# Down projections summed without the residual and without 1/rms, with x kept in device memory until the last part

## The chip, the cores and the metric

The kernel runs on one core of a Trainium2 chip. The time is the device time of one execution in microseconds, and the figure for a kernel is the median of its timed runs. Besides, one execution is recorded by the hardware profiler; its rows are quoted as they stand. The engines are named as in the profile: PE is TensorE's matrix multiplication, PEld its loading of weights, DVE is VectorE, ACT ScalarE, POOL GpSimd and SP SyncE. SP does no arithmetic here; it issues transfers, one after the other. POOL issues the transfers that add what they bring to what lies at their target.

## The reference, cut to what matters

One inference step of a decoder with two layers: 512 prompt positions and 8 sample positions, model width 1024. Layer 0 has a causal pooling mixer, layer 1 sliding-window attention, and each layer has a feed-forward network (FFN) ahead of the mixer and one behind it, four in all:

```python
def _rmsnorm(x, g):
    y = xf * lax.rsqrt(jnp.mean(xf * xf, axis=-1, keepdims=True) + EPS)
    return (y * g.astype(jnp.float32)).astype(x.dtype)

def _swiglu(x, wg, wu, wd):
    return (jax.nn.silu(x @ wg) * (x @ wu)) @ wd
...
        x = x + 0.5 * _swiglu(_rmsnorm(x, norm_g[l, 0]), ffn_w_gate[l, 0], ffn_w_up[l, 0], ffn_w_down[l, 0])
        h = _rmsnorm(x, norm_g[l, 1])
        ... mixer ...
        x = x + out
        x = x + 0.5 * _swiglu(_rmsnorm(x, norm_g[l, 2]), ffn_w_gate[l, 1], ffn_w_up[l, 1], ffn_w_down[l, 1])
```

wg and wu (Gate and Up) are 1024 x 2816, wd (Down) is 2816 x 1024. Everything is in float32.

## The kernel before

**Data.** The residual stream x stays in on-chip memory, transposed: eight tiles `x[0]` to `x[7]`, each 128 features by 520 tokens (512 and 8), 266 KB. A tile is worked on in two halves of 260 tokens. `R`, of the same shape, holds 1/rms of each token in all partitions. Since 1/rms is one factor for each token, Up's result is left without it, and the sum of Down is multiplied by `R` instead.

**Arithmetic.** A float32 matrix is split into a high and a low part (`wh` and `wl` for weights, the weight's high part by ScalarE at L260, the low one by VectorE at L261; `split`, L315, for the moving side), and a product is three matmuls: high by high, high by low, low by high. One matmul moves 128 x 260.

**An FFN** (`ffn`, L803). The 2816 hidden features are 22 tiles of 128, in three parts of 8, 8 and 6 (`PARTS`, L26). A part first makes its hidden tiles (Gate, Up, Silu, product) and then its Down, which sums over the hidden features of this part alone; so each part adds a third of the Down sum. The first two to four tiles of an FFN are computed plainly, the others by a Strassen–Winograd scheme of seven products in place of eight (`strassen_tile`), which needs sums of weight blocks. The Downs of parts 0 and 1 use the seven products as well (`strassen_down`, L727), for four pairs of x tiles, `x[2i]` and `x[2i+1]`. The Down of the last part, of six tiles, is plain; `add` (L827) puts its result into x.

**A pair in `strassen_down`.** `head`, `second`, `third` and `rest` issue the seven products (`product`, L556, matmul at L563, four weight tiles of three matmuls each) and, between them, the copies `sa` and `sb` on ScalarE (L736, L738, L744). In `third`, the sum `u` is built (L751), multiplied by `R` (L752), and `x[2i]` takes −0.5 times it (L753); `sb` takes the next product (L755). In `rest`, the two halves are multiplied by `R` (L760, L762) and `x[2i+1]` takes 0.5 times the result (L763). The signs come from the hidden values, which are kept negated. The `rest` of one pair is issued behind the head of the next, that of the last pair behind the first products of the next part's tile.

**Weights.** SP loads raw weights (L334) into three buffers (`rawp`), each as soon as VectorE's split at L261 has set a buffer free. For the Strassen sums, SP loads a block a second time into a buffer `S`; POOL adds a block to it by an accumulating transfer (L191), and another block to a block of raw (L192); VectorE makes two further sums (L197, L201). The splits run up to five pieces ahead of the products. POOL's transfers are issued in order, as SP's are.

**Order.** A scheduler reorders the instructions of an engine by its own estimate of their times, except those put into `later`, which keep the order of the text. Weight loads on SP are of that kind; the instructions of `strassen_down` on VectorE are not.

**Start of FFN 1.** Behind the pooling mixer, whose last updates of x are at L1099, the text issues on SP: a copy of the pooling state to its output (L1142), copies of the key and value caches (L1145), a load of the attention sinks (L1149) and eight small loads that spread them over partitions (L1151), all in `later`. L1180 to L1182 on VectorE turn these loads into the form that the attention uses; the text has them behind FFN 1, the scheduler puts them into its first tiles.

**Device memory.** The pool `kvp` (L1156) holds tiles in device memory, so far for keys and values.

Of the kernel before, what the change touches and what calls it, by code (L numbers as in the profile page):

```python
# [11 lines left out]
F32 = mybir.dt.float32  # L12
F32R = mybir.dt.float32r
I32 = mybir.dt.int32
AF = mybir.ActivationFunctionType
ALU = mybir.AluOpType
AX = mybir.AxisListType

P = 128
D = 1024  # L20
KT = 8
# [3 lines left out]
TOK = SP + NS  # L25
TW = TOK + NS  # L26
H = TOK // 2
PARTS = (8, 8, 6)
# [252 lines left out]
def yoco_step(ctx, tc, ins, outs):  # L281
# [9 lines left out]
    splp = ctx.enter_context(tc.tile_pool(name="splp", bufs=6))  # L291
    psp = ctx.enter_context(tc.tile_pool(name="psp", bufs=4, space=bass.MemoryType.PSUM))
    cnt = [0]

# [175 lines left out]
    def hcols(t, hf):  # L470
        return t[:, hf * H : (hf + 1) * H]


    def halves(t):
        return t.rearrange("p (h c) -> p h c", h=2)
# [250 lines left out]

    def strassen_down(tmp, hs):  # L727

# [17 lines left out]
        def third(i):  # L746
            a, c, sa, sb = st[i]
            product(b["B21"], c[:, 0, :])
            product(b["B22"], c[:, 1, :], True)
            u = tmp.tile([P, TOK], F32, tag="u", name="u", bufs=nu[0])  # L750
            V.tensor_tensor(halves(u), halves(sa), c[:, :, :H], op=ALU.add)  # L751
            V.tensor_tensor(u, u, R, op=ALU.mult)  # L752
            V.scalar_tensor_tensor(x[2 * i], u, -0.5, x[2 * i], op0=ALU.mult, op1=ALU.add)  # L753
            product(b["T3"], a, True)
            V.tensor_tensor(sb, sb, a[:, :H], op=ALU.add)  # L755

        def rest(i):
            a, c, sa, sb = st.pop(i)
            u = tmp.tile([P, TOK], F32, tag="u", name="u", bufs=nu[0])
            V.tensor_tensor(hcols(u, 1), sb, hcols(R, 1), op=ALU.mult)  # L760
            product(b["T4"], a, True)
            V.tensor_tensor(hcols(u, 0), a[:, :H], hcols(R, 0), op=ALU.mult)  # L762
            V.scalar_tensor_tensor(x[2 * i + 1], u, 0.5, x[2 * i + 1], op0=ALU.mult, op1=ALU.add)  # L763

# [38 lines left out]
    def ffn(fi, tmp, mov, hooks, tt, tags, after, before_last=None, first=None, by_parts=None, hold=False):  # L803

        j = 0
        for pi, n in enumerate(PARTS):
# [3 lines left out]
            for _ in range(n):  # L810
                if j == 0 and first is not None:
                    plain_end(tmp, *first, hs)
                elif j < NPL[fi]:
                    plain_tile(tmp, mov, hs, hooks)
                else:
                    while hooks:
                        hooks.pop(0)()
                    strassen_tile(tmp, mov, tt, hs)
                j += 1
                W.pin = lambda ins: ins  # L820
            if seven:
                strassen_down(tmp, hs)
                continue
            nk = (n + 1) // 2
            rest = NH if last and by_parts is not None else 0

            def add(m, bank, hfs):  # L827
                c = slice(hfs[0] * H, (hfs[-1] + 1) * H)
                u = tmp.tile([P, TOK], F32, tag="u", name="u", bufs=nu[0])[:, c]
                parts = lambda z: z.rearrange("p (h c) -> p h c", c=H)  # L830
                pin = later if last and hold and m == KT - 1 else seq
                pin(V.tensor_tensor(parts(u), bank[:, hfs[0] : hfs[-1] + 1, :H], parts(R[:, c]), op=ALU.mult))
                pin(V.scalar_tensor_tensor(x[m][:, c], u, -0.5, x[m][:, c], op0=ALU.mult, op1=ALU.add))

# [14 lines left out]
            for m in range(KT - rest):  # L849
                if m > 1:  # L850
                    banks[m] = duo()
                    mm_tile(hs, banks[m])
                add(m, banks[m], (0, 1))
                if last:
# [300 lines left out]

    kvp = ctx.enter_context(tc.tile_pool(name="kvp", bufs=1, space=bass.MemoryType.DRAM))  # L1156
    kT_kept = [kvp.tile([P, SP], F32, name=f"kT_kept{g}") for g in range(2)]
# [720 lines left out]
```

## Time and profile before

| | |
|---|---|
| median of 3 runs | 1652.23 us |
| lowest and highest | 1649.66 and 1653.12 us |
| profiled execution | 1657.26 us |
| its span | 1655.5 us |
| mean granted TensorE clock | 0.990 |

The stages of the profiled execution, by the first and last matmuls of each (us from the start of the span, rounded):

| | Down, part 0 | Down, part 1 | Down, last part |
|---|---|---|---|
| FFN 0 (from 9) | 108 to 146 | 230 to 268 | 325 to 372 |
| FFN 1 (from 401) | 492 to 530 | 615 to 653 | 712 to 757 |
| FFN 2 (from 776) | 864 to 902 | 986 to 1024 | 1084 to 1127 |
| FFN 3 (from 1301) | 1383 to 1421 | 1505 to 1543 | 1602 to 1656 |

The pooling mixer lies between 372 and 401 us, the attention between 1127 and 1301 us.

How to read the rows. A group row has the line, the engine, the operation, target and sources with their shapes, the count, the busy time and the mean duration in ns, and behind the second bar the idle time of the engine just before these instructions with what ended it. A row of a stretch has from and to, the length, and for each engine the busy time with the count of instructions, then the granted clock, the share of time for which the sixteen transfer engines were busy, and GB/s. A row of the timeline has start, duration, engine, line, operation and operands, and in square brackets the idle time before it with the releaser. A row of waits has who waited, for whom, and in total, times and longest. A transfer row has the queue, the count, KB each, and the median time from issue to landing.

### The profile page before, as it was taken

To read this page: it belongs to the slowest core of one execution; us is meant where nothing else is said; L and a number is where in the kernel's file an instruction comes from. 1 tells how busy PE (TensorE), PEld (TensorE's weight loads), DVE (VectorE), ACT (ScalarE), POOL (GpSimd) and SP (SyncE) were. 2 spreads that over 40 slices of the span, in tenths; PEclk is the share of its full clock that TensorE was granted. 3 is DMA by queue.
4 is the path that set the end of the run, shared out by engine and by line. 5 is a ranking of instruction groups with operands and counts; after the bars stand their busy time and mean duration, and the time that the engine had idled before them with its cause. 6 is when DMAs were issued, how large, how long until landed. Compare 5 with 4: busy or idle time off the path is not lost.

```text
span 1655.5 us, 34978 instructions
## 1 busy us (share of the span) xinstructions
PE 1624.3 (98%) x13386; PEld 1607.8 (97%) x13386; DVE 1421.8 (86%) x2817; ACT 980.1 (59%) x2032; POOL 228.9 (14%) x304
## 2 busy tenths in 40 slices
PE   9999999999999999999999999999989999999997
PEld 9999999999999999999999999999989999999997
DVE  6999999887899999888899989886786799999886
ACT  5665665566665565655655665655785565565555
POOL 1111111000111111100211111101110111111100
PEclk9999999999999999999999999999979999999999
DMA  8577878752587887744787877753222567787851
GB/s 225 119 174 180 183 175 176 192 158 87 127 181 176 179 185 176 163 134 103 186 186 178 182 175 173 170 181 91 59 50 75 126 142 176 179 184 173 178 139 52
DMA packets 377363, 254.62 MB, mean 154 GB/s; under 512 B 13134, under 2 KB 343878, under 8 KB 377156
## 3 DMA queue, kind: packets, MB, share of 16 engines
q1 hardware_dynamic: 339390, 187.30, 40.9%
q0 software_dynamic: 34048, 60.00, 22.7%
q10 hardware_dynamic: 3758, 5.09, 1.0%
q8 instruction: 105, 1.72, 0.4%
q14 instruction: 62, 0.51, 0.1%
HBM read 189.76 MB, written 6.11 MB: 118 GB/s over the span
## 4 chain that ended last, share of the span: by engine, by line
PE 90%; DVE 3%; ACT 3%; DMA 1%; issue 1%; POOL 0%; SPq 0%; DVEq 0%; ACTq 0%; POOLq 0%
PE ps L563 64%; PE ps L535 20%; ACT wh L260 1%; DVE wl L261 1%; PE ps L1464 1%; PE ps L1061 1%; DMA pr<-in_bands_dram 1%; PE ps L1086 1%; ACT sm L1408 1%; PE ps L1377 0%; PE ps L1433 0%; PE ps L494 0%; PE ps L1752 0%; PE ps L1759 0%; DMA raw<-in_ffn_w_gate_dram 0%
## 5 line engine op out<-in xcount | busy, mean ns | idle before, releaser
L260 ACT ACTIVATE wh<-raw 128x512 fp32r<-128x512 f32 (+1 forms) x794 | 465.3, 619 | 262.7 <-PE ps L535 81.3
L261 DVE TENSOR_TENSOR wl<-raw,wh 128x512 fp32r<-128x512 f32 (+1 forms) x794 | 518.0, 675 | 71.1 <-ACT wh L260 69.1
L563 PE MATMUL ps<-th,wh 128*128 128x260 f32 x1216 | 343.7, 284 | 1.5 <-ACT wh L260 1.2
L563 PE MATMUL ps<-th,wl 128*128 128x260 f32 x1216 | 342.4, 282 | 0.6 <-DVE wl L261 0.6
L563 PE MATMUL ps<-tl,wh 128*128 128x260 f32 x1216 | 342.3, 282 | 0.0
L563 PE MATMUL ps<-xh,wh 128*128 128x260 f32 x896 | 253.6, 284 | 3.3 <-ACT sb L707 1.8
L563 PE MATMUL ps<-xl,wh 128*128 128x260 f32 x896 | 251.6, 282 | 0.0
L563 PE MATMUL ps<-xh,wl 128*128 128x260 f32 x896 | 250.5, 282 | 0.5 <-DVE wl L261 0.4
L192 POOL DMA_DIRECT2D raw<-raw x108 | 93.1, 862 | 1046.8 <-DVE wl L261 283.5
L563 PEld LDWEIGHTS ps<-th,wh 128*128 128x128 f32 x1216 | 228.4, 188 | 3.7 <-ACT wh L260 2.5
L563 PEld LDWEIGHTS ps<-th,wl 128*128 128x128 f32 x1216 | 228.8, 188 | 0.8 <-DVE wl L261 0.8
L563 PEld LDWEIGHTS ps<-tl,wh 128*128 128x128 f32 x1216 | 229.0, 188 | 0.0
L563 PE MATMUL ps<-hh,wh 128*128 128x260 f32 x656 | 184.7, 285 | 2.4 <-ACT wh L260 1.8
L563 PE MATMUL ps<-hl,wh 128*128 128x260 f32 x656 | 183.8, 283 | 0.2 <-DVE hl L320 0.2
L563 PE MATMUL ps<-hh,wl 128*128 128x260 f32 x656 | 183.1, 282 | 0.0
L563 PEld LDWEIGHTS ps<-xh,wh 128*128 128x128 f32 x896 | 168.3, 188 | 5.3 <-ACT sb L707 2.2
L563 PEld LDWEIGHTS ps<-xh,wl 128*128 128x128 f32 x896 | 168.1, 188 | 0.9 <-DVE wl L261 0.9
L563 PEld LDWEIGHTS ps<-xl,wh 128*128 128x128 f32 x896 | 168.4, 188 | 0.0
L563 PEld LDWEIGHTS ps<-hh,wh 128*128 128x128 f32 x656 | 123.0, 188 | 4.3 <-ACT wh L260 2.8
L563 PEld LDWEIGHTS ps<-hl,wh 128*128 128x128 f32 x656 | 123.3, 188 | 0.4 <-DVE hl L320 0.4
L563 PEld LDWEIGHTS ps<-hh,wl 128*128 128x128 f32 x656 | 123.0, 188 | 0.0
L535 PE MATMUL ps<-hh,wh 128*128 128x260 f32 x572 | 116.3, 285 | 0.6 <-ACT vtok L1245 0.6
(331 smaller groups left out, 3595.2 us busy)
## 6 DMA issues: line engine op xcount, KB each, us to landing
raw<-in_ffn_w_gate_dram SPq DMA_DIRECT2D x87, 512.0 KB, 5.6
raw<-in_ffn_w_up_dram SPq DMA_DIRECT2D x87, 512.0 KB, 5.6
raw<-in_ffn_w_down_dram SPq DMA_DIRECT2D x128, 256.0 KB, 4.4
raw<-raw POOLq DMA_DIRECT2D x108, 256.0 KB, 3.5
S<-raw POOLq DMA_DIRECT2D x108, 256.0 KB, 4.6
S<-in_ffn_w_up_dram SPq DMA_DIRECT2D x76, 256.0 KB, 6.2
raw<-in_ffn_w_down_dram SPq DMA_DIRECT2D x16, 768.0 KB, 4.5
S<-in_ffn_w_down_dram SPq DMA_DIRECT2D x32, 256.0 KB, 4.5
```

The source lines that it names most:

```text
L192: G.dma_start(blk(raw, 2, 1), blk(raw, 1, 1), accum_op=ALU.add)
L260: pin(nc.scalar.activation(dh, src, AF.Copy))
L261: pin(nc.vector.tensor_tensor(dl, src, dh.bitcast(F32), op=ALU.subtract))
L535: ins = T.matmul(banks[:, hf, :H], a[:, kk, :], hcols(b, hf), start=(first and i == 0), stop=(last and i == 2),)
L563: T.matmul(bank[:, :H], a[:, kk, :], b, start=(not more and kk == 0 and i == 0), stop=(kk == 3 and i == 2), skip_group_check=more,)
L1061: T.matmul(o, a[:, s], b[:, kk, :], start=(n == 0), stop=(n == 5))
L1086: T.matmul(po[:, half * 256 : half * 256 + 256], z[:, tau, c], b, start=(i == 0), stop=(i == len(lst) - 1),)
L1408: S.activation(z, z, AF.Exp, scale=-1.0, bias=nm[:, i : i + 1], accum_out=self.den[:, i : i + 1])
L1464: T.matmul(po[:, bi * 256 : (bi + 1) * 256], a, p_[:, kc_], start=(n == 0), stop=(n == 3 * len(kts) - 1),)
```

## The change

For each FFN, eight tiles `kept[0]` to `kept[7]` in device memory take a copy of x. SP stores them, two behind each of the tiles 4 to 7 of the text. From then on x itself holds the bare sum of the Downs: part 0 writes it (`first`), without the sign and the factor, so that no `R` and no old x is needed; part 1 adds to it or subtracts from it. In the last part, `restore` turns x[m] into −0.5 · x[m] · `R` on VectorE, and an accumulating transfer on POOL adds `kept[m]`. The Down of the last part adds to x as it did.

```diff
+    kvp = ctx.enter_context(tc.tile_pool(name="kvp", bufs=1, space=bass.MemoryType.DRAM))
...
-    def strassen_down(tmp, hs):
+    def strassen_down(tmp, hs, first):
...
-            u = tmp.tile([P, TOK], F32, tag="u", name="u", bufs=nu[0])
+            y = x[2 * i]
+            u = y if first else tmp.tile([P, TOK], F32, tag="u", name="u", bufs=nu[0])
             V.tensor_tensor(halves(u), halves(sa), c[:, :, :H], op=ALU.add)
-            V.tensor_tensor(u, u, R, op=ALU.mult)
-            V.scalar_tensor_tensor(x[2 * i], u, -0.5, x[2 * i], op0=ALU.mult, op1=ALU.add)
+            if not first:
+                V.tensor_tensor(y, y, u, op=ALU.add)
             product(b["T3"], a, True)
-            V.tensor_tensor(sb, sb, a[:, :H], op=ALU.add)
+            if first:
+                V.scalar_tensor_tensor(hcols(x[2 * i + 1], 1), sb, -1.0, a[:, :H], op0=ALU.mult, op1=ALU.subtract)
+            else:
+                V.tensor_tensor(sb, sb, a[:, :H], op=ALU.add)
 
         def rest(i):
             a, c, sa, sb = st.pop(i)
-            u = tmp.tile([P, TOK], F32, tag="u", name="u", bufs=nu[0])
-            V.tensor_tensor(hcols(u, 1), sb, hcols(R, 1), op=ALU.mult)
+            y = x[2 * i + 1]
+            if not first:
+                V.tensor_tensor(hcols(y, 1), hcols(y, 1), sb, op=ALU.subtract)
             product(b["T4"], a, True)
-            V.tensor_tensor(hcols(u, 0), a[:, :H], hcols(R, 0), op=ALU.mult)
-            V.scalar_tensor_tensor(x[2 * i + 1], u, 0.5, x[2 * i + 1], op0=ALU.mult, op1=ALU.add)
+            if first:
+                S.activation(hcols(y, 0), a[:, :H], AF.Copy, scale=-1.0)
+            else:
+                V.tensor_tensor(hcols(y, 0), hcols(y, 0), a[:, :H], op=ALU.subtract)
...
-        j = 0
+        j, kept = 0, [kvp.tile([P, TOK], F32, name=f"x{fi}_{k}") for k in range(KT)]
+
+        def restore(m):
+            V.scalar_tensor_tensor(x[m], x[m], -0.5, R, op0=ALU.mult, op1=ALU.mult)
+            nc.gpsimd.dma_start(x[m], kept[m], accum_op=ALU.add)
+
...
                 j += 1
                 W.pin = lambda ins: ins
+                if 4 <= j < 8:
+                    for k in (2 * j - 8, 2 * j - 7):
+                        nc.sync.dma_start(kept[k], x[k])
+                if last:
+                    i = j - sum(PARTS) + n
+                    for m in range(KT * (i - 1) // n, KT * i // n):
+                        restore(m)
             if seven:
-                strassen_down(tmp, hs)
+                strassen_down(tmp, hs, pi == 0)
                 continue
```

`add` keeps its two operations (multiply by `R`, add −0.5 times it to x) and loses a parameter that had one value only. Neither the stores, nor the restoring multiplication, nor the accumulating transfer is in `later`.

More of the change, by code (lines that the diff above doesn't have):

```diff
@@ L825, in ffn, with add @@
             rest = NH if last and by_parts is not None else 0
[L827 to L833, printed above, removed]
+            def add(m, bank):
+                u = tmp.tile([P, TOK], F32, tag="u", name="u", bufs=nu[0])
+                pin = later if hold and m == KT - 1 else seq
+                pin(V.tensor_tensor(halves(u), bank[:, :, :H], halves(R), op=ALU.mult))
+                pin(V.scalar_tensor_tensor(x[m], u, -0.5, x[m], op0=ALU.mult, op1=ALU.add))
             if last and hold:
@@ L852, in ffn @@
                     mm_tile(hs, banks[m])
-                add(m, banks[m], (0, 1))
+                add(m, banks[m])
                 if last:
@@ L1153, in yoco_step @@
         ffn(1, tmp, mov2, start_hooks(tmp, 2, tt, 2), tt, HH, deferred(N_KV, tmp, "g", XX, movk))
-    kvp = ctx.enter_context(tc.tile_pool(name="kvp", bufs=1, space=bass.MemoryType.DRAM))
     kT_kept = [kvp.tile([P, SP], F32, name=f"kT_kept{g}") for g in range(2)]
```

## The prediction

> **What bounds the kernel now.** I read the busy table of the page first, then the chain of work that ended last.
>
> ```profile
> span 1655.5 us, 34978 instructions
> PE 1624.3 (98%) x13386; PEld 1607.8 (97%) x13386; DVE 1421.8 (86%) x2817; ACT 980.1 (59%) x2032; POOL 228.9 (14%) x304
> PE 90%; DVE 3%; ACT 3%; DMA 1%; issue 1%; POOL 0%; SPq 0%; DVEq 0%; ACTq 0%; POOLq 0%
> ```
>
> TensorE is busy for 98% of the span and carries 90% of the chain. The change removes no matmul, so it can gain only where TensorE waits now, and lose where it waits newly. The 1655.5 us of the span stand in an execution of 1657.26 us (1.76 around it), and that is 5.0 us above the median of 1652.23. I work out a difference on the profiled execution and add it to the median.
>
> The third view is the busy time of each engine in stretches: one stretch in which TensorE never waits, then the four Downs of part 0 (each cut in two where x is first updated, at 121.4, 506, 877 and 1398 us), then the four Downs of part 1.
>
> ```profile
> core 0: us, PE busy (x) PEld busy (x) DVE busy (x) ACT busy (x) POOL busy (x), PEclk, DMA share, GB/s
> 150.00:188.00 38.00, 38.00 (x320) 38.00 (x319) 34.50 (x65) 23.36 (x47) 6.99 (x8) 1.00 0.82 171
> 108.00:121.40 13.40, 13.07 (x104) 12.45 (x104) 13.33 (x27) 9.63 (x21) 1.74 (x3) 1.00 0.62 148
> 121.40:146.00 24.60, 24.60 (x207) 24.60 (x206) 22.99 (x43) 10.71 (x22) 5.15 (x6) 1.00 0.85 191
> 492.00:506.00 14.00, 14.00 (x119) 14.00 (x119) 13.21 (x26) 9.57 (x22) 1.72 (x2) 1.00 0.74 185
> 506.00:530.00 24.00, 23.98 (x199) 23.73 (x198) 23.14 (x43) 10.23 (x21) 5.21 (x6) 1.00 0.81 183
> 864.00:877.00 13.00, 12.72 (x103) 12.19 (x102) 12.93 (x26) 9.44 (x21) 1.72 (x2) 1.00 0.55 129
> 877.00:902.00 25.00, 25.00 (x211) 25.00 (x211) 23.47 (x43) 11.06 (x23) 5.18 (x6) 1.00 0.87 197
> 1383.00:1398.00 15.00, 14.52 (x119) 14.10 (x118) 14.04 (x28) 10.17 (x22) 2.58 (x3) 1.00 0.69 166
> 1398.00:1421.00 23.00, 23.00 (x195) 23.00 (x194) 22.02 (x41) 9.76 (x21) 4.36 (x5) 1.00 0.85 176
> ...
> 230.00:268.00 38.00, 37.31 (x311) 37.10 (x310) 36.34 (x69) 20.24 (x42) 6.90 (x8) 1.00 0.80 184
> 615.00:653.00 38.00, 36.51 (x300) 35.89 (x299) 35.44 (x67) 20.26 (x43) 6.91 (x8) 1.00 0.76 181
> 986.00:1024.00 38.00, 36.16 (x297) 35.51 (x296) 35.45 (x66) 20.87 (x43) 6.79 (x8) 1.00 0.74 174
> 1505.00:1543.00 38.00, 37.72 (x308) 36.94 (x308) 36.75 (x68) 20.60 (x44) 6.93 (x8) 1.00 0.75 180
> ```
>
> The numbers in brackets count matmuls. With no wait, 320 fit into 38 us, 0.119 us each. By that spacing the head parts of Down 0 hold 9, 0, 6 and 7 fewer than fit and the remainders 0, 3, 0 and 0: 25 slots, 3.0 us (33 slots, 3.9 us, if each of the eight stretches also counts one matmul cut by its edge). The Downs of part 1 miss 9, 20, 23 and 12 against 320: 64 slots, 7.6 us. VectorE is the fullest engine beside TensorE in these stretches (13.33 of 13.40, 12.93 of 13.00, 36.75 of 38), and the transfer engines are busy 0.74 to 0.87 of the time.
>
> **The change, part by part.** The groups of instructions of the Down function, alike in shape, are the price list (x32: four pairs, two parts, four FFNs):
>
> ```profile
> L751 DVE TENSOR_TENSOR u<-sa,ps 128x520 f32<-128x520 f32 x32 | 22.1, 690 | 5.6 <-PE ps L563 4.1 <-ACT sa L744 1.4
> L752 DVE TENSOR_TENSOR u<-u,R 128x520 f32<-128x520 f32 x32 | 22.3, 696 | 0.4
> L753 DVE SCALAR_TENSOR_TENSOR x<-u,x 128x520 f32<-128x520 f32 x32 | 22.2, 692 | 0.0
> L755 DVE TENSOR_TENSOR sb<-sb,ps 128x260 f32<-128x260 f32 x32 | 13.4, 419 | 2.8 <-PE ps L563 2.8
> L760 DVE TENSOR_TENSOR u<-sb,R 128x260 f32<-128x260 f32 x32 | 13.5, 421 | 0.0
> L762 DVE TENSOR_TENSOR u<-ps,R 128x260 f32<-128x260 f32 x32 | 13.6, 426 | 5.2 <-PE ps L563 5.0
> L763 DVE SCALAR_TENSOR_TENSOR x<-u,x 128x520 f32<-128x520 f32 x32 | 22.2, 695 | 0.3
> L736 ACT COPY sa<-ps 128x260 f32<-128x260 f32 x32 | 11.3, 371 | 21.1 <-PE ps L563 21.1
> ```
>
> *VectorE in Down 0.* A pair costs 0.690+0.696+0.692+0.419+0.421+0.426+0.695 = 4.04 us now. Afterwards the sum goes straight into x (0.69) and one half-width subtraction remains (0.42): 1.11. That is 2.93 less a pair, 11.7 an FFN, 47 us in all. But the first of it comes at the first x update, and the slots are lost ahead of that: 22 of 25. I take the 3 behind it as won (0.36 us) and a quarter of the 22 (0.65 us), since a shorter block moves some weight splits forward: −1.0 us. Bounds: 0 and −3.9.
>
> *ScalarE in Down 0.* Sixteen new half-width copies, by the nearest row (0.371) 5.9 us in all. ScalarE works about 10 us of each 24 behind the heads, and its free time hides them: nothing (0.37 us each on the path, 5.9 in all, if the left half of x were waited for at once; nobody reads it before part 1's Down).
>
> *VectorE in Down 1.* A pair becomes 0.690 (u), 0.69 (x plus u), 0.419 and two half-width subtractions of 0.42: 2.64. The restoring multiplications are issued in the last part of the program text, but in the changed program's instruction order they stand in Down 1 and the tile behind it: two a pair, 1.39. Together 4.03 against 4.04: nothing moves there. What VectorE gains, it gains in Down 0 alone.
>
> *Transfers.* Stores first: 32 of 266 KB on SP. Then 32 accumulating ones on POOL, whose nearest kin are the two of the weight sums.
>
> ```profile
> q1 hardware_dynamic: 339390, 187.30, 40.9%
> q0 software_dynamic: 34048, 60.00, 22.7%
> ...
> raw<-raw POOLq DMA_DIRECT2D x108, 256.0 KB, 3.5
> S<-raw POOLq DMA_DIRECT2D x108, 256.0 KB, 4.6
> ```
>
> The plain queue moves 187.30 MB in 40.9% of 1655.5 us: a store takes the engines for 0.96 us, 7.7 us an FFN, in the tiles at its start, where the engines are half idle (the 403 to 423 us row below, 0.46): nothing; in a full stretch it would be priced like the additions that follow. POOL's queue is almost only the 216 accumulating transfers: 22.7% of 1655.5 over 216 is 1.74 us of all sixteen engines each, 13.9 us for the eight of an FFN. In the changed order they stand among the weight sums of four chunks (x0, x1, a chunk, x2, x3, a chunk, x4 …), so they fall into the some 38 us of Down 1. Its four rows leave 0.20, 0.24, 0.26 and 0.25 of 38 us free, 9.0 us in the mean: 4.9 us too little. What that costs is bounded by 0 (the loads run ahead) and the whole backlog, 4 × 4.9 = 19.6 us. The nearest rows are a stretch that saturates today:
>
> ```profile
> 288.00:298.00 10.00, 10.00 (x86) 10.00 (x85) 7.23 (x14) 5.22 (x11) 1.96 (x3) 1.00 1.03 209
> 298.00:308.00 10.00, 10.00 (x85) 10.00 (x85) 9.73 (x18) 6.56 (x14) 0.85 (x2) 1.00 0.95 209
> ...
> 318.00:328.00 10.00, 9.98 (x83) 9.76 (x82) 9.83 (x19) 7.33 (x16) 0.00 (x0) 1.00 0.48 141
> ```
>
> Twenty microseconds at 1.03 and 0.95 are followed by 83 matmuls in place of 86: 3 × 0.119 = 0.36 us. I take 0.4 an FFN, +1.5 us.
>
> The Trainium skill speaks against the size of that term: in "DMA: Bandwidth & Descriptors", section "Anatomy of one DMA — SWDGE (gpsimd) path", a transfer issued by GpSimd takes about 2.0 us fixed and its bytes over 436 GB/s. By that, as an estimate, a 266 KB addition moves data for 0.6 us, eight would fit into the free time, and the sum would be 1.5 us lower; but POOL's own rows show 1.74 us of occupancy and 3.5 to 4.6 to landing, and those decide.
>
> *SP's queue at the start of FFN 1.* In the changed order all eight stores of FFN 1 stand ahead of the state and cache copies (L1142, L1145), the sink loads (L1151) and the next S load. SP takes its issues in order, so all of them wait for the last x of the pooling mixer. Four issues and instructions in order of time, with start and duration, and two more stretches:
>
> ```profile
> 368.88 1.08 SPq L1142 DMA_DIRECT2D out_dram<-in_state_pool_dram  x1
> ...
> 371.95 15.66 SPq L1151 DMA_DIRECT2D sink_s<-in_attn_sinks_dram  x8
> 401.89 0.74 DVE L1099 SCALAR_TENSOR_TENSOR x<-ps,gT,x 128x512 f32<-128x512 f32 x1
> ...
> 421.27 0.15 DVE L1182 TENSOR_SCALAR sink_s<-sink_s 128x1 f32<-128x1 f32 x1
> ...
> 403.00:423.00 20.00, 20.00 (x170) 20.00 (x169) 16.49 (x46) 13.12 (x25) 1.90 (x3) 1.00 0.46 103
> 438.00:449.00 11.00, 8.99 (x69) 8.15 (x68) 9.47 (x20) 8.05 (x17) 0.00 (x0) 1.00 0.00 1
> ```
>
> These issues last from 368.88 to 387.61, 18.7 us. Begun at 402.6 they end at 421.4 at the earliest, and the last sink then has to land; VectorE, in order, stands at L1182, 421.27 today, and behind it are the weight splits. The S load, issued last, is late for its sums as well. VectorE would be some 3 us late, part of which its pauses take up. Eleven microseconds later TensorE already loses slots (69 of 93). I take half of the 3, +1.5 us, between 0 and +5 (the 3 in full, and 2 more for sums that follow the late S load, an estimate).
>
> *SP elsewhere.* In FFNs 0, 2 and 3 the stores stand between weight loads.
>
> ```profile
> SPq L334 <- DVE wl L261: 854.0, 118, 24.1
> ```
>
> SP waits there 854 us for buffers that VectorE's splits set free, 7.2 us a time, and the x in question are made before those: 0. If a store waited longer than its gate, each microsecond would shorten the lead of the loads behind it by as much.
>
> Sum: −1.0 + 1.5 + 1.5 = +2.0 us; 1652.23 + 2.0 = **1654.2 us**.
>
> **Rivals.** *A, the transfers decide.* The backlog of 4.9 us an FFN meets weight sums that already arrive last:
>
> ```profile
> ACT wh L260 <- DMA S<-raw: 28.8, 13, 3.2
> ```
>
> ScalarE waits 28.8 us for these sums, in 13 places. If half the backlog reaches TensorE it is 4 × 2.45 = 9.8 us; with −1.0 and +1.5 that is +10.3: 1662.5 us, slower. For it speaks the missing 4.9 us; against it the 0.36 us after saturation. It decides from about 0.7 us lost an FFN (0.4 and a quarter of the 1.3 that part my forecast from 1655.5). The Trainium skill's "Perfetto Trace Analysis", "Identifying the Most-Contended Engine", would have transfers judged by memory bandwidth, not by occupancy of sixteen engines, which would make A unlikely; the fall to 83 behind the share of 1.03 and 0.95 speaks the other way.
>
> *B, the relief reaches TensorE.* If an emptier Down 0 keeps the heads fed (3.9 us) and shorter blocks in Down 1 (u and one addition, 1.38 us, where three operations of 2.08 stood) win a third of the 7.6 us there, 2.5, and transfers and the start of FFN 1 cost nothing, it is −6.4: 1645.8 us. For it: VectorE is full where the slots are lost. Against: the losses lie ahead of what is removed.
>
> *C, the work is only moved.* No relief in Down 0, and the restores, put by the scheduler among the splits of Down 1, raise its loss by half: +3.8, 1656.0 us. For it: VectorE at 36.75 of 38. Against: the count of operations a pair is no higher.
>
> **How the numbers follow.** The measurement tells about 0.2%, 3.3 us, from no change: faster is below 1648.9, slower above 1655.5. The forecast has 0.46 (faster 0.02, same 0.27, slower 0.17; its own range is 1651 to 1658, from −1.0 with no costs to +5 at the start of FFN 1 and +1.5), A 0.25 (slower), B 0.20 (faster 0.18, same 0.02), C 0.09 (same 0.04, slower 0.05). Totals 0.20, 0.33, 0.47. The range reaches below B and just past A's price, 1645.5 to 1664; the far halves of A and B, some 0.18, stay outside.
>
> **What would show it.** VectorE's busy time falls by some 47 us, all of it in the Downs of part 0, whose head stretches still miss slots. In the Downs of part 1 the transfer share rises towards 1, the matmul counts stay within a few of 311, 300, 297 and 308. The sinks of FFN 1 are issued after 402 us, L1182 moves to about 424, and 438 to 449 loses more. I am wrong if Down 1 falls by tens of matmuls (A), if the heads of Down 0 fill (B), or if a wait shows elsewhere: a store that holds SP's weight loads, or an addition that holds POOL's weight sums past their due time.

## The result, and the profile after

| | before | changed |
|---|---|---|
| median of 5 runs, us | 1652.23 | 1665.53 |
| lowest and highest, us | 1649.56 and 1653.9 | 1661.65 and 1672.19 |
| ratio, 95% interval | | 1.0091 (1.0062 to 1.012) |
| span of the profiled execution, us | 1655.5 | 1663.7 |

The changed kernel is slower by 0.9%, 13.3 us in the medians. The forecast was 1654.2 us, with 1664 at the upper end of its range.

The page of the changed kernel: the busy table, then the chain that ended last, by engine and by line (the matmuls of L563 are L564 here; lines below that shift too).

```profile
span 1663.7 us, 35057 instructions
PE 1621.3 (97%) x13386; PEld 1604.3 (96%) x13386; DVE 1388.2 (83%) x2737; ACT 987.3 (59%) x2048; POOL 257.1 (15%) x336
PE 77%; DMA 9%; DVE 5%; issue 4%; ACT 3%; SPq 0%; POOL 0%; ACTq 0%; DVEq 0%; POOLq 0%
PE ps L564 52%; PE ps L536 20%; DMA S<-raw 5%; DVE wl L261 2%; DMA raw<-in_ffn_w_up_dram 2%; DMA S<-in_ffn_w_up_dram 1%; ACT wh L260 1%; PE ps L1079 1%; PE ps L1104 1%; PE ps L1481 1%; DVE raw L197 1%; PE ps L1450 0%; ACT sm L1425 0%; PE ps L1769 0%; PE ps L1394 0%
```

VectorE lost 34 us of work (1421.8 to 1388.2) and the kernel became slower. TensorE's part of the chain fell from 90% to 77%; transfers took 1% before and 9% now, and over half of that is one line, S<-raw, POOL's addition into the weight sums.

The clearest reading is by stages. The same stretch of work has the same number of matmuls in both kernels, so the two lengths of it can be compared. First the tiles of the last part, in before (four FFNs), then the start of FFN 1 and the end of its part 1 with the Down:

```profile
268.00:325.00 57.00, 56.98 (x475) 56.76 (x474) 49.43 (x89) 33.80 (x68) 6.96 (x8) 1.00 0.81 179
653.00:712.00 59.00, 59.00 (x495) 59.00 (x494) 52.36 (x92) 35.56 (x70) 6.99 (x8) 1.00 0.66 156
1024.00:1084.00 60.00, 60.00 (x503) 60.00 (x502) 52.65 (x93) 35.26 (x70) 7.05 (x9) 1.00 0.69 159
1543.00:1602.00 59.00, 59.00 (x493) 58.84 (x492) 51.40 (x91) 34.73 (x70) 6.94 (x8) 1.00 0.73 160
430.00:492.00 62.00, 59.99 (x494) 59.15 (x493) 56.64 (x107) 38.15 (x76) 9.56 (x12) 1.00 0.64 139
570.00:653.00 83.00, 81.29 (x666) 79.99 (x666) 75.82 (x143) 47.15 (x97) 15.14 (x18) 1.00 0.80 182
```

The same stages in the changed kernel, in the same order, with the Down of part 1 of FFN 2 and a Down of part 0 at the end:

```profile
267.80:329.90 62.10, 58.25 (x475) 57.04 (x475) 50.21 (x90) 33.62 (x69) 10.54 (x12) 1.00 0.84 191
661.00:722.40 61.40, 59.76 (x496) 59.31 (x496) 52.04 (x92) 35.02 (x70) 12.28 (x14) 1.00 0.75 174
1032.70:1094.90 62.20, 60.52 (x503) 60.13 (x503) 52.35 (x93) 35.02 (x70) 12.28 (x14) 1.00 0.76 178
1545.80:1609.30 63.50, 59.96 (x493) 59.17 (x492) 51.29 (x91) 35.21 (x70) 11.48 (x14) 1.00 0.76 174
436.40:503.50 67.10, 62.95 (x494) 61.80 (x493) 58.45 (x110) 41.35 (x81) 9.79 (x12) 0.95 0.66 141
581.00:661.00 80.00, 79.98 (x667) 79.77 (x666) 75.14 (x141) 46.46 (x96) 15.62 (x18) 1.00 0.87 193
997.00:1032.70 35.70, 35.68 (x298) 35.48 (x297) 33.99 (x64) 19.71 (x42) 8.72 (x10) 1.00 0.89 201
108.00:145.50 37.50, 37.33 (x311) 37.12 (x311) 28.95 (x50) 22.39 (x47) 6.88 (x8) 1.00 0.71 169
```

- **The tiles of the last part** take 62.1, 61.4, 62.2 and 63.5 us where they took 57, 59, 60 and 59: +14.2 us. POOL's count of instructions there rises from 8 to 12 or 14: additions.
- **The start of FFN 1** takes 67.1 for 62.0: +5.1 us. TensorE idles for 4.15 us of it (67.10 − 62.95) where it idled for 2.01; the other 3.0 us are busy time, 62.95 for 59.99 with the same 494 matmuls, at a granted clock of 0.95 for 1.00 (third number from the end).
- **The end of part 1 and its Down** became faster: 80.0 us for 83.0 in FFN 1, 35.7 for about 38 (986 to 1024 us) in FFN 2, and about 1 us less in FFN 3; in FFN 0 the Down of part 1 is 0.6 us longer: some −6 us.
- **The Down of part 0** of FFN 0 is 0.5 us shorter, though VectorE is busy for 28.95 us where it was 36.32.

−6 + 14.2 + 5.1, with about −1 for the Downs of part 0, gives +12, near the 13.3 of the medians. The spans differ by 8.2 only, because the attention of before ran at a lower granted clock in the profiled execution (0.93) and took 7 us longer for the same 1373 matmuls. Outside the attention the two recorded executions differ by 15.0 us, so some 3 us, scattered over the last Downs, the pooling mixer and the start of FFN 2, are in none of these terms. The attention, first before, then the changed kernel:

```profile
1127.00:1301.00 174.00, 167.14 (x1373) 162.03 (x1372) 126.76 (x368) 114.08 (x301) 24.37 (x48) 0.93 0.29 71
```

```profile
1137.80:1305.00 167.20, 160.99 (x1373) 155.85 (x1372) 126.40 (x368) 113.86 (x301) 24.12 (x48) 0.97 0.33 85
```

**Where the last part waits.** POOL's timeline in the changed kernel, at the end of Down of part 1 of FFN 1 (L817 is the addition):

```profile
651.95 1.76 POOL L817 DMA_DIRECT2D x<-x  x2 [0.98 <-DVE wl L261]
663.14 0.86 POOL L192 DMA_DIRECT2D raw<-raw  x1 [9.43 <-DVE u L753]
663.68 1.22 POOL L817 DMA_DIRECT2D x<-x  x1
664.22 1.58 POOL L191 DMA_DIRECT2D S<-raw  x1
664.75 1.93 POOL L817 DMA_DIRECT2D x<-x  x1
```

and ScalarE's split of that S, on its timeline:

```profile
672.57 0.63 ACT L260 ACTIVATE wh<-S 128x512 fp32r<-128x512 f32 x1 [3.46 <-DMA S<-raw]
```

The S addition was issued at 664.22 with an x addition directly ahead of it and one behind, and 8.3 us later ScalarE had waited 3.46 us for it. TensorE then stops at 673.25 for 1.36 us. The transfers' times to landing in the changed kernel say the same over the whole run (last number; before: 4.6 for S<-raw):

```profile
S<-raw POOLq DMA_DIRECT2D x108, 256.0 KB, 5.2
x<-x POOLq DMA_DIRECT2D x32, 260.0 KB, 8.0
```

**The start of FFN 1.** SP's timeline of the changed kernel, and the two readers of what it loads late:

```profile
391.31 18.10 SPq L836 DMA_DIRECT2D x<-x  x8
...
412.36 13.52 SPq L1169 DMA_DIRECT2D sink_s<-in_attn_sinks_dram  x8
426.00 0.39 SPq L335 DMA_DIRECT2D S<-in_ffn_w_up_dram  x1
```

```profile
427.67 0.15 DVE L1199 TENSOR_SCALAR sink_s<-sink_s 128x1 f32<-128x1 f32 x1
437.59 0.63 ACT L260 ACTIVATE wh<-S 128x512 fp32r<-128x512 f32 x1 [5.59 <-DMA S<-raw]
```

The eight stores hold SP until 409.4, the sinks follow, and the S load that follows them, which in before went out right after the last sink, at 387.73, goes out at 426.00. VectorE's sink instruction (L1199, before L1182) does not wait. ScalarE stands for 5.59 us on the weight sum that needs the late S.

TensorE's waits that follow are the smaller part of the 5.1 us. Right behind them the granted clock falls to one half for 6.83 us, in which 26 matmuls run; at 0.119 us each some 57 would fit:

```profile
452.43:459.26 6.83, 6.02 (x26) 5.73 (x27) 3.54 (x8) 2.76 (x6) 0.00 (x0) 0.50 0.14 40
```

### The profile page after: what moved, and what is told of

It is laid out like the page before. It is cut to its first block, busy times and chain, and to the rows that moved or that the text cites. A ratio compares the mean times of both kernels' runs of the same rounds, so it can differ in the third digit from the quotient of the medians.

```text
span 1663.7 us, 35057 instructions
## 1 busy us (share of the span) xinstructions
PE 1621.3 (97%) x13386; PEld 1604.3 (96%) x13386; DVE 1388.2 (83%) x2737; ACT 987.3 (59%) x2048; POOL 257.1 (15%) x336
## 3 DMA queue, kind: packets, MB, share of 16 engines
q0 software_dynamic: 38656, 68.53, 25.4%
## 4 chain that ended last, share of the span: by engine, by line
PE 77%; DMA 9%; DVE 5%; issue 4%; ACT 3%; SPq 0%; POOL 0%; ACTq 0%; DVEq 0%; POOLq 0%
PE ps L564 52%; PE ps L536 20%; DMA S<-raw 5%; DVE wl L261 2%; DMA raw<-in_ffn_w_up_dram 2%; DMA S<-in_ffn_w_up_dram 1%; ACT wh L260 1%; PE ps L1079 1%; PE ps L1104 1%; PE ps L1481 1%; DVE raw L197 1%; PE ps L1450 0%; ACT sm L1425 0%; PE ps L1769 0%; PE ps L1394 0%
## 5 line engine op out<-in xcount | busy, mean ns | idle before, releaser
L564 PE MATMUL ps<-th,wh 128*128 128x260 f32 x1216 | 346.1, 285 | 12.3 <-ACT wh L260 6.6
L564 PE MATMUL ps<-tl,wh 128*128 128x260 f32 x1216 | 344.2, 283 | 0.0
L564 PE MATMUL ps<-th,wl 128*128 128x260 f32 x1216 | 343.4, 283 | 0.3 <-DVE wl L261 0.3
L564 PE MATMUL ps<-xh,wh 128*128 128x260 f32 x896 | 252.7, 284 | 3.0 <-ACT sb L708 1.4
L564 PE MATMUL ps<-xl,wh 128*128 128x260 f32 x896 | 251.6, 282 | 0.0
L564 PE MATMUL ps<-xh,wl 128*128 128x260 f32 x896 | 248.9, 282 | 2.1 <-DVE wl L261 2.0
L564 PEld LDWEIGHTS ps<-th,wh 128*128 128x128 f32 x1216 | 229.6, 189 | 16.1 <-ACT wh L260 8.1
L192 POOL DMA_DIRECT2D raw<-raw x108 | 95.6, 885 | 905.5 <-DVE wl L261 299.7
L564 PEld LDWEIGHTS ps<-th,wl 128*128 128x128 f32 x1216 | 229.8, 189 | 0.6 <-DVE wl L261 0.6
L564 PEld LDWEIGHTS ps<-tl,wh 128*128 128x128 f32 x1216 | 230.3, 189 | 0.0
L564 PE MATMUL ps<-hh,wh 128*128 128x260 f32 x656 | 184.2, 284 | 1.2 <-ACT hh L320 0.7
L564 PE MATMUL ps<-hl,wh 128*128 128x260 f32 x656 | 183.9, 282 | 0.0
L564 PE MATMUL ps<-hh,wl 128*128 128x260 f32 x656 | 182.4, 283 | 0.0
L564 PEld LDWEIGHTS ps<-xh,wh 128*128 128x128 f32 x896 | 168.3, 188 | 4.3 <-ACT sb L708 1.9
L564 PEld LDWEIGHTS ps<-xh,wl 128*128 128x128 f32 x896 | 167.4, 188 | 2.5 <-DVE wl L261 2.5
L564 PEld LDWEIGHTS ps<-xl,wh 128*128 128x128 f32 x896 | 168.5, 188 | 0.0
L191 POOL DMA_DIRECT2D S<-raw x108 | 102.2, 946 | 209.4 <-DMA S<-in_ffn_w_down_dram 46.0
L564 PEld LDWEIGHTS ps<-hh,wh 128*128 128x128 f32 x656 | 123.2, 188 | 2.0 <-ACT wh L260 0.9
L564 PEld LDWEIGHTS ps<-hl,wh 128*128 128x128 f32 x656 | 123.5, 188 | 0.0
L564 PEld LDWEIGHTS ps<-hh,wl 128*128 128x128 f32 x656 | 122.6, 188 | 0.0
```

The source lines that it names most:

```text
L191: G.dma_start(s1, blk(raw, 2, 2), accum_op=ALU.add)
L192: G.dma_start(blk(raw, 2, 1), blk(raw, 1, 1), accum_op=ALU.add)
L564: T.matmul(bank[:, :H], a[:, kk, :], b, start=(not more and kk == 0 and i == 0), stop=(kk == 3 and i == 2), skip_group_check=more,)
```

## The experiments

**Theory 1**: the additions cost because of their place, among the weight sums in POOL's order and on the transfer engines, and the stores of FFN 1 by their place on SP. **Rivals**: VectorE's new order makes the sums late; or 13.9 us of the transfer engines an FFN cost wherever they stand. The ratios are to 13 to 23 runs of the kernel before, whose median is 1653.3 to 1655.3 us; compare runs by their ratios.

### 1. No additions

```diff
         def restore(m):
             V.scalar_tensor_tensor(x[m], x[m], -0.5, R, op0=ALU.mult, op1=ALU.mult)
-            nc.gpsimd.dma_start(x[m], kept[m], accum_op=ALU.add)
```

> Leaves out the 32 accumulating transfers on POOL, so x lacks the kept residual; stores and restoring multiplications stay. Theory 1 (the additions stand among the weight sums of the last part in POOL's order and on the transfer engines, and make those late): the matmuls missing in the tiles of the last part (some 16 us over four FFNs) are there again, about 1650 us. Rival (VectorE's new order, with the restoring multiplications in it, makes the sums late): the loss stays, above 1660 us.

1652.39 us, ratio 0.9997 (0.9978 to 1.0017): the 13 us are gone with the additions. VectorE runs the same 2737 instructions in the same order as in the changed kernel, so its order is ruled out as the cause.

### 2. Multiplications and additions late

All eight `restore(m)` behind the last tile, both instructions in `later`:

```diff
-                if last:
-                    i = j - sum(PARTS) + n
-                    for m in range(KT * (i - 1) // n, KT * i // n):
+                if last and j == sum(PARTS):
+                    for m in range(KT):
                         restore(m)
```

> All eight multiplications and additions of an FFN behind its last Strassen tile, in program order, so behind all of POOL's weight sums and ahead of the plain Down, where the transfer engines are busy 0.4 to 0.6. Theory 1 (their place decides): the last part's tiles lose nothing, 1650 to 1654 us. Rival (8 x 1.74 us of the transfer engines cost wherever they stand): above 1660 us, with the loss in the last Down instead.

1669.2 us, ratio 1.0104 (1.0065 to 1.0144). Neither number was right, yet the stage named by the theory was: the tiles of the last part lost nothing, and the last Downs of FFNs 0, 2 and 3, with the norm behind, took 9, 6.5 and 4 us longer than in before. The additions' bytes alone do not explain it: run 9 moves them behind the last weight sum too, at a ratio of 1.0004. VectorE's timeline shows the eight multiplications in one block, ahead of splits for the next matmuls, and POOL can begin only then:

```profile
330.55 4.97 DVE L816 SCALAR_TENSOR_TENSOR x<-x,R 128x520 f32<-128x520 f32 x8
```

With every x late, the norm ahead of the pooling mixer is late: TensorE waits 5.67 us for its sum of squares. First this run, then before:

```profile
378.32 2.27 PE L495 MATMUL ps<-ones,acc 128*128 128x1 f32 x10 [5.67 <-DVE acc L484]
```

```profile
372.60 1.39 PE L494 MATMUL ps<-ones,acc 128*128 128x1 f32 x10 [1.65 <-DVE acc L483]
```

### 3. All stores in the order of the text

```diff
-                        nc.sync.dma_start(kept[k], x[k])
+                        later(nc.sync.dma_start(kept[k], x[k]))
```

> The stores of x are kept in the order of the text on SP, in FFN 1 behind the copies and the sink loads. Theory (SP's queue, held by the stores until the last x, makes the sinks and the S load late): the start of FFN 1 loses about 3 us again as before and not 8, so 1660 to 1661 us; the last part's tiles lose as in the changed kernel. Rival (the start of FFN 1 loses for another reason, such as the copies' own traffic or VectorE's order): 1665 us, the loss at 440 to 460 us unchanged.

1680.3 us, ratio 1.0159 (1.0117 to 1.0201), though the start of FFN 1 took 62.1 us again, as before. FFN 0 and FFN 3 lost 3.5 and 7 us in their first Strassen tiles, part of it again to a granted clock of 0.50 behind the wait (3.4 us of it from 112.3, 6.8 us from 1395.7). In FFN 0 a pair of stores now stands ahead of an S load, on SP's timeline of this run:

```profile
97.56 1.17 SPq L836 DMA_DIRECT2D x<-x  x2
98.83 0.44 SPq L335 DMA_DIRECT2D S<-in_ffn_w_down_dram  x1
```

In the changed kernel that load went out at 93.14, ahead of the raw loads.

ScalarE's timeline of this run shows the wait already met in FFN 1, for a weight sum whose S came late:

```profile
110.62 0.63 ACT L260 ACTIVATE wh<-S 128x512 fp32r<-128x512 f32 x1 [6.76 <-DMA S<-raw]
```

### 4. A plain load and an addition on VectorE

```diff
-            nc.gpsimd.dma_start(x[m], kept[m], accum_op=ALU.add)
+            u = tmp.tile([P, TOK], F32, tag="u", name="u", bufs=nu[0])
+            nc.gpsimd.dma_start(u, kept[m])
+            V.tensor_tensor(x[m], x[m], u, op=ALU.add)
```

> In the same place on POOL, a plain load of the kept tile into a spare tile and an addition on VectorE, in place of the accumulating transfer (VectorE works 22 us more). If the accumulating form is what costs (1.74 us of the engines each against 0.96 for a plain transfer of this size), a third to a half of the last part's 16 us comes back, less what VectorE's additions cost: 1658 to 1664 us. If the place in POOL's order costs whatever is moved: 1665 us or more.

1688.97 us, ratio 1.022 (1.0174 to 1.0266). The experiment did not separate what it should: POOL's timeline shows it waiting for free `u` tiles, with the weight sums queued behind, so a second wait came in:

```profile
675.88 0.54 POOL L818 DMA_DIRECT2D u<-x  x1 [6.82 <-DVE x L819]
676.42 0.91 POOL L192 DMA_DIRECT2D raw<-raw  x1
```

What the accumulating form costs beside a plain one stays open.

### 5 and 7. The additions alone moved

```diff
+                if last and j == sum(PARTS) - n + 6:
+                    for m in range(KT):
+                        later(nc.gpsimd.dma_start(x[m], kept[m], accum_op=ALU.add))
```

with the multiplications unpinned and called behind the first tile of the last part, which leaves them where the changed kernel has them on VectorE. Run 7 has in addition the edit of run 6.

> The restoring multiplications stand where they stood in the changed kernel; only the additions are moved, all eight of an FFN behind the last weight sum in POOL's order. The same bytes, the same count, another place. Theory 1 (the additions cost because they stand among the weight sums of the last part): the last part's tiles lose nothing, and as POOL is free some 15 to 20 us ahead of the last Down, that loses nothing either: 1665.5 less some 13 is 1652 us, level with before. Rival (the bytes cost wherever they stand): 1660 us or more.

> Both edits: additions behind the last weight sum, the stores of FFN 1 behind the copies. If the two costs are separate they add up: 1665.5 - 13 - 5 is 1647 us, 5 us faster than before, which is the relief in the Downs of part 1. If the second is a knock-on of the first: 1652 us.

1694.57 us (ratio 1.0238, 1.0214 to 1.0263) and 1695.39 (1.025, 1.0232 to 1.0268): the worst of all. The expectation did not describe the program. In the order that the scheduler made, the eight additions stand behind the last raw addition, but *ahead* of the last S. POOL's timeline in run 5:

```profile
703.07 0.86 POOL L192 DMA_DIRECT2D raw<-raw  x1 [7.55 <-DVE raw L197]
703.61 7.49 POOL L841 DMA_DIRECT2D x<-x  x8
712.30 0.86 POOL L191 DMA_DIRECT2D S<-raw  x1 [1.20 <-DMA x<-x]
```

The row of its waits for that releaser (total, times, longest):

```profile
ACT wh L260 <- DMA S<-raw: 72.9, 20, 11.8
```

One weight sum an FFN is behind eight additions, ScalarE waits up to 11.8 us for it, and the tiles of the last part take 69.5 us in FFN 1 in place of 59. Of the ten, 6.9 are waits of TensorE; 3.6 are longer busy time for the same matmuls (62.62 for 59.00), since behind the wait the granted clock is 0.50 for 10.2 us. A misread order became the sharpest test of the queue: same bytes, same count, one S late, ten microseconds an FFN. Run 7 had the start of FFN 1 back at 62.1 us and lost 5.6 us in the Down of part 0 that follows: ScalarE waits 7.09 us there for a weight sum, and the granted clock is 0.50 for 3.4 us behind it. Why that sum is late in run 7 and not in run 6 stays open.

### 6. Only the stores of FFN 1 pinned

```diff
-                        nc.sync.dma_start(kept[k], x[k])
+                        st = nc.sync.dma_start(kept[k], x[k])
+                        if fi == 1:
+                            later(st)
```

> Only the stores of FFN 1 are kept in the order of the text, behind the copies and sink loads; the rest as in the changed kernel. Theory (SP's queue at the start of FFN 1 costs 5 us, the pinned stores of the other FFNs cost the rest in the earlier run): 1660 to 1661 us. Rival (pinning costs in every FFN): 1668 us or more.

1665.25 us, ratio 1.0078 (1.0049 to 1.0107). The start of FFN 1 took 62.1 us in place of 67.1, as expected; the median hardly moved, since in the profiled run the start of FFN 2 and the last part of FFN 3 took some 1.7 us more each (in the latter the granted clock is 0.50 for 3.4 us, in the changed kernel it is not), and the interval cannot tell 1.0078 from 1.0091. Alone this run settles little; run 10 beside run 9 does.

### 8. Half the bytes

```diff
-            nc.gpsimd.dma_start(x[m], kept[m], accum_op=ALU.add)
+            nc.gpsimd.dma_start(x[m][:, :H], kept[m][:, :H], accum_op=ALU.add)
```

> Adds only the left half of each kept tile (the right half of x lacks its residual): the same count and places on POOL, half the bytes. If the transfer engines' time is what makes the weight sums late, about half of the 13 us comes back or more: 1655 to 1659 us. If each addition costs by its issue and its place in the queue: 1664 us or more.

1659.09 us, ratio 1.0036 (1.002 to 1.0052). With as many issues, in the same places and as long on POOL (1.30 us each, 1.26 in the changed kernel), more than half of the loss to run 1 came back (0.0055 of 0.0094). So the larger part of the delay goes with the additions' data and not with their issue; what the rest goes with, this run does not show.

### 9. The additions really behind the last S

As in run 5, and POOL's weight sums pinned too, in the order raw, S:

```diff
-            G.dma_start(s1, blk(raw, 2, 2), accum_op=ALU.add)
-            G.dma_start(blk(raw, 2, 1), blk(raw, 1, 1), accum_op=ALU.add)
+            self.pin_home(G.dma_start(blk(raw, 2, 1), blk(raw, 1, 1), accum_op=ALU.add))
+            self.pin_home(G.dma_start(s1, blk(raw, 2, 2), accum_op=ALU.add))
```

> POOL's two transfers of each weight sum are kept in the order of the text, so the eight additions of an FFN now really stand behind the last S of the FFN in POOL's order (in the run before they stood ahead of it), and the multiplications where the changed kernel has them. Theory 1 (the place on POOL's queue decides): the last part's tiles lose nothing, the last Down loses less than in the run where multiplications and additions were both late, as the additions start some 20 us earlier: 1665.5 less 12 to 14 is 1651 to 1654 us. Rival (the 13.9 us of the transfer engines cost an FFN something at any place): 1658 us or more, lost in the last Down.

1654.63 us, ratio 1.0004 (0.999 to 1.0017). POOL's timeline (L192 is now S, L191 raw), and then the stretch of the last part's tiles, in FFN 1:

```profile
696.52 1.21 POOL L192 DMA_DIRECT2D S<-raw  x1
697.06 7.85 POOL L841 DMA_DIRECT2D x<-x  x8
```

```profile
658.10:717.10 59.00, 59.00 (x495) 59.00 (x494) 52.18 (x92) 35.11 (x70) 14.23 (x17) 1.00 0.92 196
```

All additions run within these 59 us, the transfer engines are busy for 0.92 of them, more than in the changed kernel (0.75), and TensorE loses nothing; only FFN 0 loses, 58.3 us for 57.0. The bytes are the same as in run 5, where this stage took 69.5 us, and VectorE, ScalarE and TensorE run their instructions in the changed kernel's order. That is theory 1 against both rivals.

### 10. Both places put right

Run 9, and in FFN 1 all eight stores in `later` behind its second tile, which on SP is behind the sinks and the S load:

```diff
+                if fi == 1 and j == 2:
+                    for k in range(KT):
+                        later(nc.sync.dma_start(kept[k], x[k]))
-                if 4 <= j < 8:
+                if fi != 1 and 4 <= j < 8:
```

> The same, and the stores of FFN 1 in the text's order right behind the sink loads, ahead of the weight loads of tiles 2 and up. If the two costs are separate: 5 us less than the run beside it, 1646 to 1649 us, so 4 to 6 us faster than before, all of it in the Downs of part 1. If the stores cost wherever they stand in FFN 1: no better than the run beside it.

1648.97 us, ratio 0.9968 (0.9956 to 0.9981): faster than before and than the changed kernel. 0.0036 lies between it and run 9, 6 us, for the one edit in FFN 1. In the recorded executions the start of FFN 1 itself is 4.1 us shorter: 62.1 us at a granted clock of 1.00, where run 9 has 66.2 at 0.95.

The clock falls to 0.50 in this stage in every run that has these stores ahead of the sinks (the changed kernel and runs 1, 2, 4, 5, 8, 9 and 11), and stays at 1.00 in every run that has them behind (3, 6, 7, 10 and 12), as in before. No run changes the clock alone; that the longer waits bring it down is read from their order in time.

### 11. Part 1's block on VectorE as long as before

```diff
             if not first:
+                V.tensor_tensor(u, u, R, op=ALU.mult)
                 V.tensor_tensor(y, y, u, op=ALU.add)
```

> The changed kernel with one more 128x520 multiplication by R (0.70 us) between the sum u and its addition to x in part 1 (x is then wrong by that factor): the block on VectorE in each pair of part 1's Down is as long as before, 2.08 us. Theory (the shorter block ahead of the weight splits is what frees the Downs of part 1): those Downs miss matmuls again as before, about 6 us over the four FFNs, 1671 us. Rival (the relief comes from VectorE's being further ahead after the lighter Down of part 0): the Downs of part 1 stay full, 1665 us.

1667.11 us, ratio 1.0068 (1.0046 to 1.0091), which cannot be told from the changed kernel. The same matmuls of the Down of part 1 of FFN 2 take 0.5 us more than in the changed kernel, of the 2.4 that it had won on before. The length of that block explains little of the relief.

### 12. Down 0 as heavy as before

Run 10, with VectorE given back 2.93 us in each pair of part 0's Down (two multiplications of x[2i] by `R`, two halves and one whole of x[2i+1]; part 1 is as in run 10):

```diff
+            if first:
+                V.tensor_tensor(y, y, R, op=ALU.mult)
+                V.tensor_tensor(y, y, R, op=ALU.mult)
             product(b["T3"], a, True)
...
+            if first:
+                V.tensor_tensor(hcols(y, 1), hcols(y, 1), hcols(R, 1), op=ALU.mult)
             product(b["T4"], a, True)
...
                 S.activation(hcols(y, 0), a[:, :H], AF.Copy, scale=-1.0)
+                V.tensor_tensor(hcols(y, 0), hcols(y, 0), hcols(R, 0), op=ALU.mult)
+                V.tensor_tensor(y, y, R, op=ALU.mult)
```

> The kernel with both edits, and in each pair of part 0's Down multiplications by R put back on VectorE (three of 128x520, two of 128x260, 2.93 us: what the change took out there; x is then wrong by powers of R). Part 1 is untouched. Theory (VectorE, lightened in Down 0, stays ahead through part 1 and frees its Down): the matmuls missing in part 1's last tiles and its Downs are missing again, some 6 us, and the time goes from 1649 back to 1654 to 1656 us. Rival (part 1's own shorter operations free it): the Downs of part 1 stay full, only Down 0 may lose some, 1649 to 1651 us.

1653.77 us, ratio 0.9998 (0.9983 to 1.0013): the gain of run 10 is gone. First the end of part 1 with its Down in FFN 1, and the Down of part 1 in FFN 2, of run 10; then the same stages of run 12:

```profile
573.80:653.80 80.00, 79.99 (x666) 79.71 (x665) 75.07 (x141) 46.34 (x96) 13.59 (x16) 1.00 0.83 182
986.80:1022.30 35.50, 35.49 (x296) 35.28 (x295) 33.82 (x63) 19.58 (x42) 5.63 (x7) 1.00 0.74 180
```

```profile
570.70:653.10 82.40, 81.18 (x667) 80.11 (x666) 75.26 (x142) 47.10 (x97) 14.80 (x18) 1.00 0.79 179
989.30:1025.60 36.30, 35.54 (x296) 35.23 (x295) 34.18 (x64) 19.50 (x41) 6.38 (x8) 1.00 0.78 180
```

No line of part 1 was changed, and it lost 2.4 and 0.8 us, 80 to 120 us behind the padded Down. So the relief in part 1 hangs on what is done in Down 0. It does not follow that VectorE carries a lead through part 1, because the built order of part 1 changed as well: the scheduler, given other work in Down 0, laid out VectorE, ScalarE and TensorE anew. At the first pair of the Down of part 1 in FFN 2, VectorE has the addition to x right behind the sum `u` in run 10 and two weight splits between them in run 12:

```profile
997.76 0.69 DVE L753 TENSOR_TENSOR u<-sa,ps 128x520 f32<-128x520 f32 x1
998.49 0.70 DVE L755 TENSOR_TENSOR x<-x,u 128x520 f32<-128x520 f32 x1
```

```profile
1001.66 0.69 DVE L753 TENSOR_TENSOR u<-sa,ps 128x520 f32<-128x520 f32 x1
1002.26 1.29 DVE L261 TENSOR_TENSOR wl<-raw,wh 128x512 fp32r<-128x512 f32 x2
1003.47 0.69 DVE L755 TENSOR_TENSOR x<-x,u 128x520 f32<-128x520 f32 x1
```

A lead of VectorE and another order are not separated by any run. In FFN 3 the Down of part 1 did not lose again, and 1.8 of the 5.0 us between the two recorded executions lie outside these two stages (the starts of FFN 2 and FFN 3 each took some 1.5 us more, ahead of their own padded Downs), so not all of the relief is accounted for.

## Why the prediction was wrong, step by step

- **VectorE in Down 0, −1.0 us.** Right in size (about −1): most of the lost slots stayed lost. That VectorE worked 7 us less of 38 there and TensorE hardly noticed is what the step said. The rows of the changed operations lost the 47 us that were forecast (129.3 to 82.3 us); the page's busy time, in which overlapping instructions count once, fell by 34.
- **VectorE in Down 1, "nothing moves there".** The price was right (the work is equal), the conclusion wrong: part 1's end and its Downs gained some 6 us. The step that failed looked at the work within each stage and took a stage for closed. Run 12 shows that a good part of the relief goes when the work of Down 0 comes back; whether through VectorE's lead or through the order that the scheduler then builds stays open. Rival B had the size of the relief (6.4 us; measured 7 with Down 0), but most of it in Down 0, and in Down 1 by its shorter block, which run 11 makes unlikely.
- **Transfers, +1.5 us.** This step failed; measured it is +14 us. The occupancy of 13.9 us was near: POOL's queue took 25.4% of 1663.7 us in the changed kernel, 46.8 us more than in before, 11.7 an FFN. The place was not: in FFN 1 four of the eight additions are issued within Down 1 and four behind its end, and the transfer share in FFN 2's Down 1 is 0.89, so the 4.9 us were not missing there. Mis-sized was the price, taken from a row behind 20 us of saturation at 1.03 and 0.95 (not right behind: from 308 to 318 us all 86 matmuls run). That row shows the engines full, not a weight sum behind other transfers in POOL's queue. The prediction named just that, an addition that holds POOL's weight sums past their due time, as a sign of being wrong, without a price. Run 9 has the stage at 0.92 with no loss, run 5 the same stage at 0.80 with 10 us of loss: what decides is which transfers stand ahead of the next S.
- **Rival A** was the right mechanism, weight sums arriving late, priced 9.8 us against 14 and with its place a stage early: the Downs of part 1 stayed full (but for 0.6 us in FFN 0), and the loss came in the tiles behind, where the sums issued around its end are used. The note quoted from the Trainium skill, "DMA: Bandwidth & Descriptors", "Anatomy of one DMA — SWDGE (gpsimd) path", by which, as an estimate, eight additions would move their data in 4.9 us, is not what the runs show: with 2.0 us fixed, one would land after 2.6 us; the additions landed after 8.0 in the median, and an S behind eight of them kept ScalarE waiting up to 11.8 us.
- **SP at the start of FFN 1, +1.5 us.** Mechanism right; measured 5.1 us, of which 2.1 are waits, within the step's bounds, and 3.0 are the granted clock of 0.50 behind them, a term that the prediction put at nothing. The queue was held longer than reckoned, as the stores themselves keep SP until 409.4 where the step began at 402.6. VectorE at L1182 was named first and does not wait; the S load, priced as an afterthought, makes ScalarE wait 5.59 us, and ScalarE, in order, holds every split behind it. Run 10 has both back, the waits and the clock.
- **Stores elsewhere, 0.** Held in the changed kernel to within a microsecond; run 3 shows for FFN 0 that it holds because the scheduler put them behind the S loads.
- **Rival C** fell: run 1 has the restoring multiplications where the changed kernel has them, and its Downs of part 1 are all shorter than before's.
- **Two readings** are off and move no term: the heads of Down 0 have transfer shares of 0.55 to 0.74, not 0.74 to 0.87, and the stretch from 438 us that already loses slots begins 17 us behind L1182, not eleven.

The terms came out at −7, +14 and +5 where the sum had −1.0, +1.5 and +1.5: the signs right, the sizes too small on both sides. That the measured time lies only 1.5 us above the range of 1645.5 to 1664 is luck: the relief in part 1, which the sum did not have, took back almost half of what the additions cost.

## What to carry to other kernels

Price an extra transfer by what stands behind it on its in-order queue and when that is due, not by whether the transfer engines have time: the same 32 additions cost nothing measurable behind the last weight sum (run 9), 0.9% of the time among the sums, and 2.4% with all eight of an FFN ahead of one sum (run 5), each against run 1. Read the built order of that queue before naming a place; one S on the wrong side of eight additions turned the remedy into the worst run. A wait of TensorE can cost more than its length: look at the granted clock behind it, which in the changed kernel made 5.1 us out of 2.1. And work taken out of one stage can change the time of a later one, through a lead or through the order that a scheduler builds from it; padding the first stage changes both, so it does not tell them apart.

## What the runs showed of the hardware that was not expected

- Eight accumulating transfers of 260 KB issued in a row take POOL 7.5 to 7.9 us to issue and land 11 to 12 us after their issue in the median (runs 5 and 9), against 8.0 when spread out in the changed kernel and 3.5 to 4.6 for a weight sum in before.
- A stretch with the transfer engines busy 0.92 of 59 us cost TensorE nothing (run 9), one at 0.80 of 69.5 us cost ten microseconds (run 5): occupancy alone said nothing of the loss.
- Behind TensorE's waits the granted clock was 0.50 for 6.83 us at the start of FFN 1 (from 452.43, the changed kernel) and for 10.24 us in the last part of FFN 1 (from 721.20, run 5).
- The same 1373 matmuls of the attention took 174.0, 167.2 and 166.4 us at granted clocks of 0.93, 0.97 and 1.00 (before, the changed kernel, run 10), which is enough to hide half of this change's effect in a pair of single profiles.
